# Preparing the first y and gate tiles within the scan stage, and holding a quarter of a long convolution's taps back behind the first attention heads, in a two-block kernel

## The chip, the cores and the metric

The kernel runs on one core of a Trainium2 chip. The metric is device time in microseconds for one execution; the figure given for a kernel is the median of several. Besides the timed runs there is one profiled execution, with a time of its own, from which all rows below are read. Engines: PE is TensorE's matrix products, PEld its weight loads, DVE is VectorE, ACT is ScalarE, POOL is GpSimd, SP is SyncE, which here issues all transfers.

## What is computed

A sequence of 512 tokens with 1024 features passes through two blocks. The first has an RWKV-7 mixer and a short-convolution mixer, the second a branch with a 31-tap causal depthwise convolution beside stick-breaking attention, then a feed-forward part. What the change touches is this:

```python
# first block, RWKV-7 mixer, after the scan over chunks and the group norm
y = (y + bonus.reshape(bsz, t, D_INNER)) * jax.nn.silu(g.astype(f32))
out = y.astype(h.dtype) @ w_out                    # 512x2048 @ 2048x1024
...
# second block
u = jax.nn.glu(conv_in, axis=-1)
u = causal_depthwise_conv(u, conv_dw_w, conv_dw_b) # 31 taps, 512 channels
u = jax.nn.silu(layernorm(u, conv_ln_g, conv_ln_b))
conv_out = jnp.einsum('bsc,cd->bsd', u, w_conv_branch) + b_conv_branch
att = stick_breaking_attention(q, k, v)            # 8 heads of 64, 128-row query blocks
att_out = jnp.einsum('bsc,cd->bsd', att, w_att_branch)
merged = jax.nn.sigmoid(g_conv) * conv_out + jax.nn.sigmoid(g_att) * att_out
```

## The kernel before

Every dense product is done with both operands split into a high and a low part (`split`, L175 to L178: ScalarE casts the high part at L176, VectorE subtracts it at L177), and three matmuls per pair of tiles: high by high, high by low, low by high. A weight chunk of 128 x 1024 numbers is fetched by SyncE (`Products.fetch`, L60), cast by ScalarE (L65), and its low part made by POOL in two halves (L73). TensorE's three matmuls are L85 to L87 in `dense_feat` and L119 to L121 in `dense_tok`.

The program has stages one after the other. `scan_phase` runs the chunked scan over 8 pairs of head tiles (q = 0 to 7); it lists operations with a cost, a due time and dependencies, and `list_schedule` orders them over the engines. Pair q stores two tiles of y, 128 x 512 each, to `yD` (L1408). In between, 16 gate tiles are computed (L1466 to L1473) and stored to `sgD` (L1476). The gate products read `xg`, which fills the shared slots 2 and 3 until the last of them; the slots 0 and 1 hold the scan's `g` by turns.

`post_phase` begins with the output projection. `prep(c)` (L1793) loads two of the sixteen tiles of y and of the gate (`yl`, `gl`, L1796, three buffers each), multiplies them on VectorE (L1797) and splits the product into `y2`: the first eight tiles lie in slots 2 and 3, the others in `yb`. `out_proj` calls it before each weight chunk, runs a first pass of 16 row tiles (12 matmuls each) over half of the output columns, and a second pass over the other half. At c = 2 prep also issues the loads of the norm's gain and of x (L1659, L1802).

Later `post_phase` does the long convolution (L1877 to L1889): for each of four channel tiles the GLU product goes to `up`, one instruction starts `conv` with tap 0 (L1884), and thirty more add a tap each on VectorE (L1887). `attention` (L2021) takes eight heads. `scores(hd)` makes z = k q^T (L2035), then on ScalarE Abs, Exp and Ln (L2042 to L2044), on VectorE ez (L2046), on POOL the mask (L2047), and the split into `sp` (L2049, L2050). `weights(hd)` adds the running sums of sp to z (L2064), then VectorE takes a minimum (L2067), ScalarE exponentiates (L2068, L2070), VectorE masks (L2071), and `pat` collects the values (L2072). The buffer of ez is doubled, so the third and fourth blocks of a head wait for the first two.

Between these steps stand fillers, other work for TensorE: g is a gate product (24 matmuls), b a convolution branch (12), n the convolution's layer norm, a its activation. A string for each head says what comes ahead of the next head's scores, ahead of the weights, and behind them. The engines' queues are in order; the framework's own scheduler merges the calls into one order for each engine.

Of the kernel before, what the change touches and what calls it, by code (L numbers as in the profile page):

```python
# [17 lines left out]
P = 128  # L18
T = 512
NT = T // P  # L20
D = 1024
KD = D // P
DI = 2048
KI = DI // P

C = 64
NC = T // C
# [4 lines left out]
CW2 = 31  # L32
# [120 lines left out]
def two_block_kernel(ctx, tc, A, out):  # L153
    nc = tc.nc
# [104 lines left out]
    with ExitStack() as rk_ctx:  # L259
# [28 lines left out]
        shared = dict(xg=[], VU=[])  # L288
# [303 lines left out]
def emit_ops(nc, tc, ops, bufs):  # L592
    ET = mybir.EngineType
    order = list_schedule(ops, bufs)
    with tc.manual_schedule(engines={ET.PE, ET.DVE, ET.Activation, ET.Pool, ET.SP}):
        for o in order:
            o["fn"]()
# [486 lines left out]
def scan_phase(nc, tc, A, E):  # L1084
# [5 lines left out]
    op = L.op  # L1090
    Q = KI // 2
    with ExitStack() as s:
# [402 lines left out]

        for q in range(Q):
            build(q)
        gate()
        emit_ops(nc, tc, L, dict(KB=2, ZR=4, V=1, VU=4, m=3, G=4, KBT=4, wy=1, UU=2, **INVERSE,
# [136 lines left out]
def post_phase(ctx, tc, A, out, E):  # L1636
# [147 lines left out]
    with ExitStack() as s:  # L1784
        gp = s.enter_context(tc.tile_pool(name="gp", bufs=1))
        ep = s.enter_context(tc.tile_pool(name="ep", bufs=1))
        gain = gain_tile(ep, "b_norm", load=False)
        ya = (slot(2), slot(3))
        yb = tuple(gp.tile([P, KD, T], F32R, tag=f"yb{i}", name=f"yb{i}") for i in range(2))
        y2 = tuple(rows(a) + rows(b) for a, b in zip(ya, yb))  # L1790

        def prep(c):
            for i in (2 * c, 2 * c + 1):  # L1793
                y, g = (ep.tile([P, T], F32, tag=n, name=n, bufs=3) for n in ("yl", "gl"))
                for t, src in ((y, yD), (g, sgD)):
# [60 lines left out]
    with ExitStack() as s:  # L1856
# [8 lines left out]
        with tc.tile_pool(name="mq", bufs=1) as mq:  # L1865
# [12 lines left out]
            vt = mq.tile([P, NT, T], F32, tag="vt", name="vt")  # L1878
            for i in range(4):
# [6 lines left out]
                for tap in range(1, CW2):  # L1886
                    nc.vector.scalar_tensor_tensor(out=conv[:, i, :], in0=up[:, i, tap:tap + T],  # L1887
                                                   scalar=col("conv_dw_w_2", tap * 4 + i), in1=conv[:, i, :],
                                                   op0=ALU.mult, op1=ALU.add)  # L1889
# [48 lines left out]
            def conv_branch(i):  # L1938
# [6 lines left out]
            todo = dict(g=gates, b=branches, n=iter([conv_norm]), a=iter([conv_act]))  # L1945
            filler = [[[next(todo[q]) for q in part] for part in head.split(",")] for head in
                      ("ggg,g,", ",ng,", "a,g,g", ",g,bb", ",g,b", ",g,ggbb", ",g,gb", ",g,gbb")]
# [72 lines left out]
def attention(nc, tc, E):  # L2020
    qT, kT, vt, at, mq, bank, filler = (E[k] for k in ("qT", "kT", "vt", "at", "mq", "bank", "filler"))  # L2021
# [4 lines left out]
    def scores(hd):  # L2026
# [4 lines left out]
        for i in (0, 1, 3, 2):  # L2031
# [18 lines left out]
            nc.vector.tensor_tensor(out=lo, in0=sp, in1=hi.bitcast(F32), op=ALU.subtract)  # L2050
        heads[hd] = zs, sps

    def weights(hd):
# [6 lines left out]
        for i in range(NT):  # L2060
# [10 lines left out]
            nc.vector.tensor_tensor(out=a[:, 0:P], in0=a[:, 0:P], in1=cmask, op=ALU.mult)  # L2071
# [41 lines left out]
```

## Time and profile before

| | us |
|---|---|
| timed runs, median (lowest to highest of 3) | 2073.43 (2072.57 to 2083.99) |
| profiled execution, its own time | 2071.24 |
| its span, first to last instruction | 2069.5 |
| busy: PE / DVE / ACT / POOL | 1967.4 / 1046.2 / 838.8 / 760.7 |
| mean granted TensorE clock | 0.980 |

The span lies inside the execution's own time, 1.7 us shorter. Times of rows count from the span's start. A clock of 1.00 in a row is TensorE's higher level, 2.4 GHz, and 0.50 the lower, 1.2 GHz; values between are stretches with both. A matmul's row shows its length with pipelining, so one that follows another starts earlier than the other's end. The chain of work that ended last is 77% PE and 13% DVE, the convolution's taps alone 6%.

### The profile page before, as it was taken

Reading aid. Unit: us, or ns where it says so; the run is one execution under the profiler, and the core shown is the slowest. Engines: PE = TensorE matmul, PEld = TensorE weight load, DVE = VectorE, ACT = ScalarE, POOL = GpSimd, SP = SyncE. Lnnn points to the kernel's source line nnn. Section 1 sums busy time; section 2 is a strip of 40 time slices with the busy share of each in tenths; the row PEclk is TensorE's granted clock in tenths of the full one; section 3 lists DMA queues with packets and bytes.
Section 4 is the critical chain, followed back from the end, with each engine's and each line's share of the span. In section 5 each row is a group of like instructions: output and inputs, shape, how many; then the busy total and the mean of one; then the engine's idle time right before and its main releaser. Section 6 shows DMA issues by size and latency. Waiting matters only on the chain.

```text
span 2069.5 us, 37138 instructions
## 1 busy us (share of the span) xinstructions
PE 1967.4 (95%) x15076; PEld 1579.5 (76%) x15076; DVE 1046.2 (51%) x2007; ACT 838.8 (41%) x1637; POOL 760.7 (37%) x660
## 2 busy tenths in 40 slices
PE   6989999799999979999999999996999999999998
PEld 5768888587778758888888887884667778888886
DVE  7958987688785342432332313797552442111101
ACT  5444554376655632322222223323765343223221
POOL 4220000001001135555555556753233565544442
PEclk9999999899999989999999999998999999999999
DMA  4445555634443383333333333331111523333321
GB/s 150 121 167 184 190 191 174 184 115 147 142 131 105 107 285 113 89 96 93 98 95 93 100 114 102 112 93 45 33 50 51 167 73 102 92 94 100 102 93 70
DMA packets 285763, 241.14 MB, mean 117 GB/s; under 512 B 14520, under 2 KB 236056, under 8 KB 285592
## 3 DMA queue, kind: packets, MB, share of 16 engines
q1 hardware_dynamic: 285592, 238.77, 37.2%
q8 instruction: 118, 1.93, 0.4%
q14 instruction: 53, 0.43, 0.1%
HBM read 198.89 MB, written 39.85 MB: 115 GB/s over the span
## 4 chain that ended last, share of the span: by engine, by line
PE 77%; DVE 13%; DMA 3%; issue 3%; ACT 2%; POOL 2%; SPq 0%; DVEq 0%; POOLq 0%; ACTq 0%
PE b L86 11%; PE b L85 11%; PE b L87 11%; PE b L120 6%; PE b L121 6%; DVE conv L1887 6%; PE b L119 5%; PE ps_d L940 3%; PE ps_d L941 3%; PE ps_d L942 3%; PE wy L1206 2%; PE us L1206 2%; PE ps_g L1466 1%; DVE X L662 1%; DVE xtmp L654 1%
## 5 line engine op out<-in xcount | busy, mean ns | idle before, releaser
L73 POOL TENSOR_TENSOR wl<-wr,wh 128x512 fp32r<-128x512 f32 (+1 forms) x463 | 641.4, 1408 | 615.1 <-ACT wh L65 613.8
L65 ACT CAST wh<-wr 128x1024 fp32r<-128x1024 f32 (+1 forms) x241 | 245.5, 1020 | 706.7 <-PE b L86 475.2
L87 PE MATMUL b<-s,wl 128*128 128x512 f32 x1024 | 404.1, 395 | 0.0
L86 PE MATMUL b<-s,wh 128*128 128x512 f32 x1024 | 404.0, 395 | 0.0
L85 PE MATMUL b<-s,wh 128*128 128x512 f32 x1024 | 403.1, 394 | 0.0
L85 PEld LDWEIGHTS b<-s,wh 128*128 128x128 f32 x1024 | 192.6, 188 | 47.0 <-issue 1.5
L86 PEld LDWEIGHTS b<-s,wh 128*128 128x128 f32 x1024 | 192.7, 188 | 45.7 <-issue 1.4
L87 PEld LDWEIGHTS b<-s,wl 128*128 128x128 f32 x1024 | 192.9, 188 | 43.6 <-issue 0.8
L119 PE MATMUL b<-wh,s 128*128 128x512 f32 x288 | 115.1, 400 | 13.9 <-ACT s L176 13.9
L1887 DVE SCALAR_TENSOR_TENSOR conv<-up,pkC,conv 128x512 f32<-128x512 f32 x120 | 117.1, 1042 | 0.4
L1359 POOL TENSOR_SCALAR var<-var 128x8 f32<-128x8 f32 x16 | 4.7, 293 | 305.9 <-ACT scr L1352 305.9
L120 PE MATMUL b<-wl,s 128*128 128x512 f32 x288 | 114.7, 398 | 0.0
L121 PE MATMUL b<-wh,s 128*128 128x512 f32 x288 | 111.1, 397 | 0.0
L2006 DVE TENSOR_TENSOR a<-sg,b 128x512 f32<-128x512 f32 x22 | 15.1, 688 | 172.5 <-PE b L87 164.3
L119 PEld LDWEIGHTS b<-wh,s 128*128 128x128 f32 x288 | 54.8, 190 | 27.8 <-ACT s L176 15.0
L1827 DVE TENSOR_TENSOR cu<-b,us 128x512 f32<-128x512 f32 x16 | 11.1, 692 | 124.3 <-PE b L87 119.0
L869 POOL MEMSET sg<- 128x8 f32 x16 | 1.7, 112 | 180.8 <-ACT pcl L893 162.7
L662 DVE TENSOR_TENSOR X<-X,xtmp 128x120 f32<-128x120 f32 (+24 forms) x248 | 65.0, 262 | 6.0
L654 DVE TENSOR_TENSOR xtmp<-dn,X 128x120 f32<-128x120 f32 (+24 forms) x248 | 64.8, 261 | 5.9
L121 PEld LDWEIGHTS b<-wh,s 128*128 128x128 f32 x288 | 54.8, 190 | 13.1
L120 PEld LDWEIGHTS b<-wl,s 128*128 128x128 f32 x288 | 54.8, 190 | 12.9
L1466 PE MATMUL ps_g<-xg_hi,wh 128*128 128x512 f32 x128 | 58.7, 459 | 2.0 <-ACT sgt L1473 2.0
(346 smaller groups left out, 4132.5 us busy)
## 6 DMA issues: line engine op xcount, KB each, us to landing
wr<-in_a_w_in SPq DMA_DIRECT2D x64, 512.0 KB, 4.6
wr<-in_b_w_in SPq DMA_DIRECT2D x64, 512.0 KB, 4.1
wr<-in_w_ffn_up SPq DMA_DIRECT2D x44, 512.0 KB, 3.9
wr<-in_w_in SPq DMA_DIRECT2D x36, 512.0 KB, 3.7
wr<-in_w_ffn_down SPq DMA_DIRECT2D x22, 512.0 KB, 3.5
kbD<-KB SPq DMA_DIRECT2D x16, 512.0 KB, 2.8
zrD<-ZR SPq DMA_DIRECT2D x16, 512.0 KB, 3.4
KB<-kbD SPq DMA_DIRECT2D x16, 512.0 KB, 4.5
```

What stands on the lines that cost most here:

```text
L65: copy = self.nc.scalar.copy(out=hi[:, :n], in_=raw[:, :n])
L73: eng.tensor_tensor(out=lo[:, sl], in0=raw[:, sl], in1=hi[:, sl].bitcast(F32), op=ALU.subtract)
L85: nc.tensor.matmul(ps, wh[:, k, :], xh[k], start=k == 0, stop=False)
L86: nc.tensor.matmul(ps, wh[:, k, :], xl[k], start=False, stop=False)
L87: nc.tensor.matmul(ps, wl[:, k, :], xh[k], start=False, stop=k == nk - 1)
L119: nc.tensor.matmul(pss[t], th, wh[:, k, :], start=s, stop=False)
L120: nc.tensor.matmul(pss[t], th, wl[:, k, :], start=False, stop=False)
L121: nc.tensor.matmul(pss[t], tl, wh[:, k, :], start=False, stop=e)
L654: nc.vector.tensor_tensor(out=tmp(i), in0=S["dn"][:, :, i:i + 1, 0:i].to_broadcast([P, 2, w, i]), in1=S["X32"][:, :, c:, i:i + 1].to_broad ...
L662: nc.vector.tensor_tensor(out=X, in0=X, in1=tmp(i), op=ALU.subtract)
L1206: nc.tensor.matmul(out, lhs, rhs, start=start, stop=True, skip_group_check=True)
L1887: nc.vector.scalar_tensor_tensor(out=conv[:, i, :], in0=up[:, i, tap:tap + T], scalar=col("conv_dw_w_2", tap * 4 + i), in1=conv[:, i, :], ...
```

## The change

There are two parts. In the scan stage a new `first_rows` loads the first four tiles of y and gate into slot 0, after the last use of that slot by pair 6, multiplies them on VectorE, and, after the last gate product has read slots 2 and 3, splits them into these slots. `prep` then does only tiles 4 to 15. In the second block the thirty taps of the fourth channel tile no longer follow its tap 0; six fillers c of five taps each are called in heads 0 to 2, and a tap may stand on VectorE only behind the last `sp` or mask operation that was called before it (`mark`). The layer norm n moves from head 1 to head 3, the activation a from head 2 to head 4, and gates and branches are dealt anew.

```diff
+        def first_rows():
...
+                    for b, src in enumerate((yD, sgD)):
+                        nc.sync.dma_start(out=S["in"][:, 2 * i + b, :], in_=src[i * P:(i + 1) * P, :])
...
+                    nc.vector.tensor_tensor(out=y, in0=y, in1=S["in"][:, 2 * i + 1, :], op=ALU.mult)
...
+                    nc.scalar.copy(out=made[0][:, i, :], in_=S["in"][:, 2 * i, :])
...
+                    nc.vector.tensor_tensor(out=made[1][:, i, :], in0=S["in"][:, 2 * i, :],
+                                            in1=made[0][:, i, :].bitcast(F32), op=ALU.subtract)
...
+            for i in range(4):
+                op("SP", 0.4, ld(i), 40 + i, ("y", "ld", i), [(Q - 2, "y_add", NC - 1)] + ([("y", "ld", 0)] if i else []),
+                   dma=2.0)
+                op("DVE", 0.69, gated(i), 40 + i, ("y", "gated", i), [("y", "ld", i)])
+                op("ACT", 0.6, high(i), 40 + i, ("y", "high", i),
+                   [("y", "gated", i), (100 + KI - 1, "dense", 7)] + ([("y", "high", 0)] if i else []))
+                op("DVE", 0.69, low(i), 40 + i, ("y", "low", i), [("y", "high", i)])
...
-        ya = (slot(2), slot(3))
+        ya = E["shared"]["y2"]
...
-            for i in (2 * c, 2 * c + 1):
+            for i in (2 * c, 2 * c + 1) if c > 1 else ():
...
+            def taps(i, which):
+                for tap in which:
+                    y = nc.vector.scalar_tensor_tensor(out=conv[:, i, :], in0=up[:, i, tap:tap + T],
...
+                    if mark:
+                        after(y, mark[-1])
...
-                for tap in range(1, CW2):
-                    nc.vector.scalar_tensor_tensor(out=conv[:, i, :], in0=up[:, i, tap:tap + T],
-                                                   scalar=col("conv_dw_w_2", tap * 4 + i), in1=conv[:, i, :],
-                                                   op0=ALU.mult, op1=ALU.add)
+                if i < 3:
+                    taps(i, range(1, CW2))
...
+            rest = iter([partial(taps, 3, range(t, t + 5)) for t in range(1, CW2, 5)])
...
-                      ("ggg,g,", ",ng,", "a,g,g", ",g,bb", ",g,b", ",g,ggbb", ",g,gb", ",g,gbb")]
+("ggg,cg,c", "c,cg,g", "c,cg,g", ",ng,g", "a,g,g", ",g,bbg", ",g,bbb", ",g,bbb")]
...
-            nc.vector.tensor_tensor(out=lo, in0=sp, in1=hi.bitcast(F32), op=ALU.subtract)
+            mark.append(nc.vector.tensor_tensor(out=lo, in0=sp, in1=hi.bitcast(F32), op=ALU.subtract))
...
-            nc.vector.tensor_tensor(out=a[:, 0:P], in0=a[:, 0:P], in1=cmask, op=ALU.mult)
+            mark.append(nc.vector.tensor_tensor(out=a[:, 0:P], in0=a[:, 0:P], in1=cmask, op=ALU.mult))
```

How the order moves, at three places. SyncE in the last pair of the scan, as a piece of the difference (L1505 are the new loads, L1476 a gate store, L1445 the last gate tile's weights, L743 V, L1408 the y store of pair 6):

```order
-L1476 DMA sgD<-sgt 128x512
-L1445 DMA wr<-in_a_w_in 128x8x128
-L743 DMA V<-vD 64x4x128 x4
+L1505 DMA y_in<-yD 128x512
+L1505 DMA y_in<-sgD 128x512
+L1476 DMA sgD<-sgt 128x512
+L1505 DMA y_in<-yD 128x512
+L1505 DMA y_in<-sgD 128x512
+L1445 DMA wr<-in_a_w_in 128x8x128
+L1505 DMA y_in<-yD 128x512
+L1505 DMA y_in<-sgD 128x512
+L743 DMA V<-vD 64x4x128 x4
```

Three of the four pairs of loads stand ahead of the V loads; the fourth follows them, and the y stores of pairs 6 and 7 come later still.

ScalarE at the end of the scan (L1473 evicts the last gate tile, L1397 scales the last rows of y, L1519 is the new cast of the high part, L176 the cast in `prep`):

```order
 L65 CAST wh<-wr 128x1024 x2
 L1473 ACTIVATE sgt<-ps_g 128x512
-L1397 ACTIVATE yo<-tY,pkB 128x256 x2
-L176 CAST s_9868<-yl 128x512 x3
```

That is the order before: no cast of a y tile ahead of the last rows of y, and `prep` begins with tile 0. The same place in the change:

```order
+L1519 CAST y_hl_9843<-y_in 128x512
+L1397 ACTIVATE yo<-tY,pkB 128x256 x2
+L1519 CAST y_hl_9843<-y_in 128x512 x3
+L176 CAST y_hl_9843<-yl 128x512
+L65 CAST wh<-wr 128x1024
```

One new cast goes ahead of the last rows of y, three behind them, and the first cast in `prep` is now that of tile 4.

VectorE at the first attention head, before (L1887 taps, L2046 ez, L2050 the low part of sp):

```order
1474 L1884 TENSOR_SCALAR conv<-up,pkC,pkB 128x512
1475 L1887 SCALAR_TENSOR_TENSOR conv<-up,pkC,conv 128x512 x82
1476 L2046 SCALAR_TENSOR_TENSOR ez<-z,ez 128x512
1477 L2046 SCALAR_TENSOR_TENSOR ez<-z_14578,ez 128x384
1478 L2050 TENSOR_TENSOR sp_14588<-ez,sp_14587 128x512
```

All taps of the block stand ahead of the first ez. In the change, at the same place (L1925 taps, L2097 ez, L2101 the low part, L2118 the minimum, L2122 the mask):

```order
1479 L1936 TENSOR_SCALAR conv<-up,pkC,pkB 128x512
1480 L1925 SCALAR_TENSOR_TENSOR conv<-up,pkC,conv 128x512 x52
1481 L2097 SCALAR_TENSOR_TENSOR ez<-z,ez 128x512
1482 L2097 SCALAR_TENSOR_TENSOR ez<-z_14541,ez 128x384
1483 L2101 TENSOR_TENSOR sp_14551<-ez,sp_14550 128x512
```

The block ahead of the first ez is 30 taps shorter. Where the 30 stand now, a piece from heads 1 and 2:

```order
1502 L2101 TENSOR_TENSOR sp_14737<-ez,sp_14736 128x256
1503 L1925 SCALAR_TENSOR_TENSOR conv<-up,pkC,conv 128x512
1504 L2122 TENSOR_TENSOR ea<-ea,cmask 128x128
1505 L1925 SCALAR_TENSOR_TENSOR conv<-up,pkC,conv 128x512 x2
1506 L2097 SCALAR_TENSOR_TENSOR ez<-z,ez 128x512
1507 L1925 SCALAR_TENSOR_TENSOR conv<-up,pkC,conv 128x512
1508 L2097 SCALAR_TENSOR_TENSOR ez<-z_14834,ez 128x384
1509 L1925 SCALAR_TENSOR_TENSOR conv<-up,pkC,conv 128x512
1510 L2101 TENSOR_TENSOR sp_14844<-ez,sp_14843 128x512
```

They stand one to three at a time behind the last low part of head 1's scores (row 1502), the last of them behind the weights of head 2.

## Rows read from the trace of the kernel before

**Rows 1.** List of waits of the whole execution: waiting engine and line, total us, times, longest.

```profile
PE z L2035 <- DVE ez L2046: 21.6, 2, 20.6
PE b L119 <- ACT s L176: 13.9, 3, 11.3
```

**Rows 2.** Timeline of TensorE, 727 to 789: start us, us, instruction, idle before and its releaser.

```profile
727.29 0.33 PE L1383 MATMUL tY<-ident,Y 128*128 128x128 f32 x1 [0.33 <-ACT Y L1367]
738.89 0.79 PE L119 MATMUL b<-wh,s 128*128 128x512 f32 x1 [11.27 <-ACT s L176]
744.07 0.39 PE L119 MATMUL b<-wh,s 128*128 128x512 f32 x1
755.52 0.51 PE L119 MATMUL b<-wh,s 128*128 128x512 f32 x1 [1.70 <-ACT s L176]
788.92 0.39 PE L119 MATMUL b<-wh,s 128*128 128x512 f32 x1
```

**Rows 3.** Timeline of ScalarE, VectorE and SyncE, 729 to 738, same columns.

```profile
729.51 1.00 ACT L1397 ACTIVATE yo<-tY,pkB 128x256 f32<-128x256 f32 x2
730.10 0.88 DVE L1403 TENSOR_TENSOR yo<-tV,yo 128x256 f32<-128x256 f32 x2 [9.51 <-ACT yo L1397]
737.45 0.69 DVE L1797 TENSOR_TENSOR yl<-yl,gl 128x512 f32<-128x512 f32 x1 [6.48 <-DMA gl<-sgD]
733.65 0.32 SPq L1796 DMA_DIRECT2D yl<-yD  x1
```

**Rows 4.** Table by stage: stretch, length, busy by engine, granted clock, DMA share, GB/s.

```profile
730.00:745.00 15.00, 6.11 (x17) 4.84 (x18) 4.85 (x8) 2.37 (x5) 3.17 (x3) 0.54 0.94 319
745.00:755.00 10.00, 7.86 (x33) 5.75 (x31) 2.83 (x4) 2.77 (x4) 2.96 (x2) 1.00 1.01 380
```

**Rows 5.** Timeline of VectorE in the last pair's scan, one step of eight.

```profile
692.75 0.29 DVE L1263 TENSOR_TENSOR UU<-us,sums 128x128 f32<-128x128 f32 x1 [1.97 <-PE us L1206]
```

**Rows 6.** VectorE's taps: chain, timeline, and table by stage (PE, PEld, DVE, ACT, POOL).

```profile
1312.58 1.69 DVE conv L1887
...
1358.14 45.30 DVE L1887 SCALAR_TENSOR_TENSOR conv<-up,pkC,conv 128x512 f32<-128x512 f32 x43
...
1410.08 21.90 DVE L1887 SCALAR_TENSOR_TENSOR conv<-up,pkC,conv 128x512 f32<-128x512 f32 x32
...
1358.10:1403.40 45.30, 45.30 (x194) 36.14 (x193) 45.30 (x45) 13.30 (x18) 25.64 (x16) 1.00 0.33 100
```

**Rows 7.** TensorE at the first attention head: timeline, and table by stage.

```profile
1433.10 0.79 PE L2035 MATMUL z<-qT,kT 64*128 64x128 f32 x2 [20.64 <-DVE ez L2046]
...
1436.00:1438.00 2.00, 2.00 (x8) 1.58 (x8) 0.00 (x0) 1.97 (x8) 1.78 (x2) 0.79 0.00 0
```

**Rows 8.** The attention stage: table by stage, and groups of instructions over 1420 to 1660.

```profile
1450.00:1475.00 25.00, 24.62 (x116) 16.70 (x116) 16.84 (x47) 16.53 (x45) 8.13 (x14) 1.00 0.08 22
...
L2050 DVE TENSOR_TENSOR sp<-ez,sp 128x512 fp32r<-128x512 f32 (+3 forms) x32 | 20.2, 645 | 8.1 <-ACT sp L2049 7.9
L2046 DVE SCALAR_TENSOR_TENSOR ez<-z,ez 128x512 f32<-128x512 f32 (+3 forms) x32 | 15.1, 485 | 26.9 <-ACT ez L2044 26.8
L2071 DVE TENSOR_TENSOR ea<-ea,cmask 128x128 f32<-128x128 f32 x32 | 15.1, 476 | 8.0 <-ACT ea L2068 7.8
L2067 DVE TENSOR_SCALAR ea<-z 128x128 f32<-128x128 f32 x32 | 9.3, 290 | 37.0 <-PE z L2064 23.1 <-PE pat L2072 13.9
L2072 PE MATMUL pat<-ea,vt 128*64 128x512 f32 (+3 forms) x64 | 25.0, 481 | 0.2 <-DVE ea L2071 0.2
L2035 PE MATMUL z<-qT,kT 64*128 64x128 f32 (+3 forms) x58 | 21.7, 485 | 22.1 <-DVE ez L2046 21.6 <-DVE ea L2067 0.5
L2064 PE MATMUL z<-sp,tri_neg 128*128 128x512 f32 (+3 forms) x64 | 19.2, 363 | 0.0
L2064 PE MATMUL z<-sp,ones_neg 128*128 128x128 f32 (+2 forms) x96 | 17.5, 284 | 0.0
```

**Rows 9.** Table by stage in the fourth head.

```profile
1516.00:1518.00 2.00, 2.00 (x3) 0.44 (x3) 2.00 (x2) 0.59 (x3) 2.00 (x3) 0.50 0.00 0
```

More of the change, by code (lines that the diff above doesn't have):

```diff
@@ L287, in two_block_kernel @@
         iv = rk_ctx.enter_context(tc.tile_pool(name="iv", bufs=1))
-        shared = dict(xg=[], VU=[])
+        shared = dict(xg=[], VU=[], y2=[])
         chunk_phase(nc, tc, A, locals())
@@ L1494, in gate, with ld, go, gated @@
                 tile_ops(i)
+        def first_rows():
+            S, made = {}, E["shared"]["y2"]
+            def ld(i):
+                def go():
+                    if i == 0:
+                        S["in"] = rc.tile([P, KD, T], F32, tag="s0", name="y_in")
+                    for b, src in enumerate((yD, sgD)):
+                        nc.sync.dma_start(out=S["in"][:, 2 * i + b, :], in_=src[i * P:(i + 1) * P, :])
+                return go
+            def gated(i):
+                def go():
+                    y = S["in"][:, 2 * i, :]
+                    nc.vector.tensor_tensor(out=y, in0=y, in1=S["in"][:, 2 * i + 1, :], op=ALU.mult)
+                return go
+            def high(i):
+                def go():
+                    if i == 0:
+                        for b in range(2):
+                            made.append(rc.tile([P, KD, T], F32R, tag=f"s{2 + b}", name=f"y_hl{b}"))
+                    nc.scalar.copy(out=made[0][:, i, :], in_=S["in"][:, 2 * i, :])
+                return go
+            def low(i):
+                def go():
+                    nc.vector.tensor_tensor(out=made[1][:, i, :], in0=S["in"][:, 2 * i, :],
+                                            in1=made[0][:, i, :].bitcast(F32), op=ALU.subtract)
+                return go
+            for i in range(4):
[5 more added lines that the diff above has]
+                op("DVE", 0.69, low(i), 40 + i, ("y", "low", i), [("y", "high", i)])
         for q in range(Q):
@@ L1498, in scan_phase @@
         gate()
+        first_rows()
         emit_ops(nc, tc, L, dict(KB=2, ZR=4, V=1, VU=4, m=3, G=4, KBT=4, wy=1, UU=2, **INVERSE,
@@ L1878, in post_phase @@
             vt = mq.tile([P, NT, T], F32, tag="vt", name="vt")
+            mark = []
+            def taps(i, which):
+                for tap in which:
+                    y = nc.vector.scalar_tensor_tensor(out=conv[:, i, :], in0=up[:, i, tap:tap + T],
+                                                       scalar=col("conv_dw_w_2", tap * 4 + i), in1=conv[:, i, :],
+                                                       op0=ALU.mult, op1=ALU.add)
+                    if mark:
+                        after(y, mark[-1])
             for i in range(4):
@@ L1944, in post_phase @@
             branches = iter([partial(conv_branch, i) for i in range(KD)])
-            todo = dict(g=gates, b=branches, n=iter([conv_norm]), a=iter([conv_act]))
+            rest = iter([partial(taps, 3, range(t, t + 5)) for t in range(1, CW2, 5)])
+            todo = dict(g=gates, b=branches, c=rest, n=iter([conv_norm]), a=iter([conv_act]))
             filler = [[[next(todo[q]) for q in part] for part in head.split(",")] for head in
-                      ("ggg,g,", ",ng,", "a,g,g", ",g,bb", ",g,b", ",g,ggbb", ",g,gb", ",g,gbb")]
+("ggg,cg,c", "c,cg,g", "c,cg,g", ",ng,g", "a,g,g", ",g,bbg", ",g,bbb", ",g,bbb")]
             attention(nc, tc, locals() | E)
@@ L2020, in attention @@
 def attention(nc, tc, E):
-    qT, kT, vt, at, mq, bank, filler = (E[k] for k in ("qT", "kT", "vt", "at", "mq", "bank", "filler"))
+    qT, kT, vt, at, mq, bank, filler, mark = (E[k] for k in ("qT", "kT", "vt", "at", "mq", "bank", "filler", "mark"))
     tri_neg, ones_neg, cmask, split, table, after = (E[k] for k in ("tri_neg", "ones_neg", "cmask", "split", "table",
```

## Prediction

> **What bounds the kernel now.** I read the list of waits first, because TensorE is busy nearly all the time and only its few long waits can be won. Two single waits stand out [rows 1]: one of 20.6 us for VectorE at the first attention head (z of L2035, behind ez of L2046), and one of 11.3 us for ScalarE at the head of the first output projection (L119, behind the cast of L176). The timelines around the two places then say what ended each wait, and the table by stage says what the clock did.
>
> The first place [rows 2]: the scan's last transposes end at 727.62, and the projection starts at 738.89. Between them ScalarE and VectorE finish the last rows of y, y is stored, the loads of y and gate go out behind that store at 733.65, their gating starts at 737.45, and only the cast after it lets TensorE go [rows 3]. The granted clock is then 0.54 over 730 to 745 [rows 4], the lower level, 1.2 GHz, for over half of that stretch. Two smaller waits for the same loads follow. From 755.52 to 788.92 the pass is unbroken: 12 of its 16 row tiles in 33.40 us, 2.78 us a tile [rows 2]. The transfers bind in the middle: 319 GB/s over 730 to 745 and 380 over the ten us behind, with the queues busy 0.94 and 1.01 of the time [rows 4].
>
> The second place: VectorE runs the 120 taps of the long convolution in one block that ends at 1431.98 [rows 6], and the first head's ez, in program order behind them, is what z waits for until 1433.10 [rows 7]. TensorE has nothing else it may do, since its queue is in order.
>
> **The change, part one: four y tiles in the scan.** Eight loads move out of the projection's head into the last pair of the scan. They are past the point where they could wait for the last y store, since SyncE's order has them ahead of it. SyncE's issues are 0.32 to 0.43 us each (the row of 733.65 is one), about 3 us for eight; behind them on SyncE stand a gate store, the last gate weights and the V loads, so these may go out some 3 us later in sum, spread over three places. VectorE gets four products of 0.69 us in the scan's steps. It sits idle 1.97 us in front of a scan product there [rows 5], so each fits; if a load were late, the scan step behind it would wait as long. I take nought, between a loss of 3 us (four products all in the way) and a gain of 1 us (VectorE's order now has one scan step ahead of a product that waits for V).
>
> At the end, four casts of 0.62 us and four low parts of 0.69 us (those of the rows behind 737.45) wait for the last gate matmul, whose input lies in the slots that they write. One cast stands ahead of the last two ScalarE operations on y, so these move from 729.51 to 730.1, and VectorE's additions from 730.10 to 730.7, ending at 731.6 with their 0.88 us [rows 3]. TensorE's first product waits for VectorE and starts at about 731.8, not 738.89; it needs only tile 0, and the three other tiles, 0.62 us of ScalarE each, stay ahead of its 2.78 us a tile. Its wait is still some 4 us, so I let the clock drop as it did before: 12 products then took from 738.89 to 744.07, 5.2 us in place of 2.8, a loss of 2.4. I keep that loss whole (bounds 0 and 2.4).
>
> Tiles 0 to 3 last until 731.8 + 4 x 2.78 + 2.4 = 745.3, tiles 4 and 5 until 750.9. Their loads start where those of tiles 0 and 1 did, half a us later, and were through in 4 us then. Tile 6 comes behind one weight chunk, four loads of y and gate, the gain, four loads of x and its own two: 4.5 MB from about 733.5, at 319 GB/s over 14 us, so by 748, gated and cast by 750. It is about in time; I take 0.7 us of waiting, between 0 and 5 (the far bound is a rate of some 230 GB/s, under both stretches of [rows 4]). From there a tile with its half chunk of weights is 0.75 MB per 2.78 us, 270 GB/s, below what the queues moved. The pass ends at 731.8 + 16 x 2.78 + 2.4 + 0.7 = 779.4 in place of 788.92: **9.5 us** less, bounds 4 and 12.5.
>
> **Part two: thirty taps behind the first heads.** With POOL idle the last 32 taps take 21.90 us, 0.684 each. So the last 30 start at 1431.98 - 30 x 0.684 = 1411.4 [rows 6]; that is when VectorE now comes to the head's ez. The two ez that TensorE waits for take to 1412.6, and z goes at 1412.8 in place of 1433.10. ScalarE and POOL sat idle behind the same wait, and their next casts and low parts start as much earlier. That is **20.3 us**. Behind the old wait the clock was still at the lower level until about 1436.8 (0.79 over 1436 to 1438 [rows 7]), half of 3.7 us: **1.9 us** more, since the new wait is under half a us.
>
> What comes back: 30 taps among the operations of heads 1 to 3, between the last scores of head 1 and the last weights of head 2. VectorE's own work there is two heads. The four lines of a head (L2050, L2046, L2071, L2067) sum to 59.7 us for eight heads, 7.5 us a head [rows 8]. A tap beside POOL is dearer: 43 taps took 45.30 us where POOL was busy 25.64 of 45.30 us, 1.05 each against 0.684 [rows 6]. Linear in POOL's share, 0.33 in the heads [rows 8], a tap is 0.684 + 0.37 x 0.33/0.57 = 0.90 us. Sum for VectorE: 27 + 15 = 42 us. TensorE in that stretch has four gate products of 24 matmuls at 0.232 us (2.78 over the 12 of a tile), 22.3, and two heads at (25.0 + 21.7 + 19.2 + 17.5)/8 = 10.4 us, 43 in all [rows 8]. So the two engines are level, and the cover is thin. VectorE enters with a lead, because a gate of 5.6 us stands on TensorE ahead of what reads head 1's last scores. I take 1.5 us of new waits, between 0 and 23 (below).
>
> The gates and branches are also dealt anew: a head has at least two of the 5.6 us gates as cover, where head 1 had one gate and head 4 one and a half. Around 1516 the before ran at a clock of 0.50 [rows 9] after waits of under 1 us; such a loss is some 4 to 5 us. It may go, stay or come elsewhere, since branches move late: I take 1.5 us gained, between a gain of 5 and a loss of 3.
>
> A rule speaks against this part. The rows say 1.05 us beside a POOL busy 0.57 of the time [rows 6], which is 0.62 of POOL's time added to VectorE's. The Trainium skill (SBUF — State Buffer, section Who interferes with whom) says that a VectorE instruction with two SBUF inputs and a GpSimd instruction that reads SBUF exclude each other: whichever starts first holds the port for its whole length. By that rule all of POOL's time would be added, a tap would be 0.684/0.67 = 1.02 us, VectorE's sum 45.6 and the total some 2 to 3 us later; the trace agrees in kind and not in full.
>
> **Sum.** 9.5 + 20.3 + 1.9 - 1.5 + 1.5 = 31.7 us. Against the profiled execution's 2071.24 us that is 2039.5; against the median of the runs shown, 2073.43, which is 2.2 above it, 2041.7. I forecast **2041** for a median.
>
> **The rivals.**
> 1. VectorE becomes the bound in heads 1 to 3. For it: 42 against 43 us, and the first taps of the block, beside an always busy POOL, took 1.69 us (one of four alike stands in [rows 6]). At that price it is 50.7 + 15 = 65.7 us, 22.7 over TensorE's 43; at 1.05 it is 3.6 over. Against it: POOL's share there is 0.33. Middle: 12 us back, 2053. Chance 0.16.
> 2. The transfers keep the gain of part one. For it: the queues were full from 730 to 755 [rows 4], and x and the gain still stand ahead of tile 6. With tile 6 some 5 us late part one is 4: 2047. Against it: 2 MB less in that stretch. Chance 0.13.
> 3. The wait at the first head is only passed on: its chain (three ScalarE passes, ez, mask, cast, low part, twice for want of buffers) becomes the wait once VectorE is free. Half of the 20.3 us comes back: about 2052 to 2055. Against it: after 1433.10 TensorE ran on without a wait over the same chain. Chance 0.03.
> 4. Slower: taps in front of each head's operations make TensorE stop for under 1 us again and again, as around 1516, and the clock stays at 1.2 GHz through all of that stretch. Its 43 us of work then cost 86: 2041 + 43 = 2084. It decides once the lower level holds for over 32 us of work. Against it: the old gaps there lasted one head. Chance 0.02.
> That the change does not act is excluded by the order: loads and taps stand where the diff says.
>
> **How the numbers follow.** Forecast 0.66, with an own range of 2033 to 2050; rivals 0.16, 0.13, 0.03 and 0.02. The range of 2030 to 2058 takes in the gains' far bounds below (12.5, and 5 more in the late heads) and most of rival 1 above. One per cent, 20.7 us, is about what a measurement of this kernel can tell from no change: under 2052.7 lie nearly all of the forecast and of rival 2 and half of rival 1, 0.85; within one per cent 0.13; slower 0.02.
>
> **What would show it.** Right: a first projection matmul near 732, second pass at about 779; no wait over 2 us for ez at the first head, taps ending near 1402 (1411.4 less 9.5), and TensorE near full over the next three heads. Wrong: a long wait of L119 for y tiles 6 or 7; VectorE at 0.95 or more with TensorE waiting for sp or ea through heads 1 to 3; a clock of 0.50 in windows there; a scan that ends later than 727.6.

## The result and the profile after

The changed kernel took 2043.86 us (median of 4 runs, 2039.32 to 2045.16), the kernel before 2074.09 in the runs beside it (2072.57 to 2083.99): a ratio of 0.9838, 95% interval 0.9820 to 0.9856, some 30 us or 1.6% less. Forecast were 2041 and a range of 2030 to 2058. The profiled execution has a span of 2041.8 us and took 2043.54.

From the list of waits of the changed kernel over the whole execution, the rows of the projection and of the attention; columns as in [rows 1]:

```profile
PE b L119 <- DVE yo L1403: 4.5, 1, 4.5
...
PE b L119 <- ACT y_hl L176: 2.0, 1, 2.0
...
PE pat L2123 <- DVE ea L2122: 0.9, 1, 0.9
PE z L2086 <- DVE ez L2097: 0.8, 1, 0.8
```

Both long waits of [rows 1] are gone. At the head of the first projection TensorE waits 4.5 us where it waited 11.3, and no longer for a y tile but for its own PSUM bank, which VectorE's last addition of y frees. At the first attention head it waits 0.8 us for ez where it waited 20.6.

The timeline of TensorE around the projection, against [rows 2]:

```profile
729.01 0.33 PE L1383 MATMUL tY<-ident,Y 128*128 128x128 f32 x1 [0.34 <-ACT Y L1367]
733.83 0.77 PE L119 MATMUL b<-wh,y_hl 128*128 128x512 f32 x1 [4.49 <-DVE yo L1403]
755.58 0.50 PE L119 MATMUL b<-wh,y_hl 128*128 128x512 f32 x1 [1.98 <-ACT y_hl L176]
824.72 1.03 PE L1724 MATMUL tp<-ident,xg 128*128 128x128 f32 x8
```

The last row is the first transpose behind the whole projection, the same point in both programs. In the kernel before it is this one:

```profile
828.64 0.60 PE L1683 MATMUL tp<-ident,xg 128*128 128x128 f32 x4
```

So the profile has only 3.9 us gained at the end of the projection. But the scan ended at 729.34 here and at 727.62 before. From the end of the scan to that transpose it is 95.38 us against 101.02: part one gained 5.6 us in this pair of profiles, and 1.7 us of it are covered by a scan that was longer in this execution. Ten profiles of kernels with the early y tiles (this one and nine of those below) have the scan's end between 724.54 and 735.07, mean 729.4; the two without have it at 727.62 and 730.39. The early loads and products do not cause the delay. At the same transposes, about when the first early load goes out (675.67 in the kernel before, 678.01 here), the changed kernel was already 2.3 us late. From there to the scan's end it took 51.3 us, the kernel before 52.0; in the other kernels with early tiles that stretch is 50.0 to 51.5 us, in part two alone 52.4. From here on the places are measured each from its own start.

Why it is 5.6 and not more shows in the other engines' timelines (ScalarE, VectorE, SyncE) of the changed kernel over the same stretch:

```profile
728.87 1.97 ACT L65 CAST wh<-wr 128x1024 fp32r<-128x1024 f32 x2
730.75 0.58 ACT L1473 ACTIVATE sgt<-ps_g 128x512 f32<-128x512 f32 x1
731.74 1.01 ACT L1397 ACTIVATE yo<-tY,pkB 128x256 f32<-128x256 f32 x2
...
731.87 1.14 DVE L1524 TENSOR_TENSOR y_hl<-y_in,y_hl 128x512 fp32r<-128x512 f32 x1 [9.27 <-ACT y_hl L1519]
732.94 0.74 DVE L1403 TENSOR_TENSOR yo<-tV,yo 128x256 f32<-128x256 f32 x2
754.18 0.69 DVE L1838 TENSOR_TENSOR yl<-yl,gl 128x512 f32<-128x512 f32 x1 [6.09 <-DMA gl<-sgD]
...
738.75 0.32 SPq L1837 DMA_DIRECT2D yl<-yD  x1
741.01 3.08 SPq L1843 DMA_DIRECT2D x_sb<-in_x  x4
745.03 0.67 SPq L1837 DMA_DIRECT2D gl<-sgD  x1
```

And the chain of waits there, start and length of each piece:

```profile
733.81 4.80 DMA yD<-yo
738.75 4.09 DMA yl<-yD
...
745.03 9.12 DMA gl<-sgD
```

In the kernel before, the first of these pieces reads:

```profile
731.00 2.51 DMA yD<-yo
```

One of the new low parts (731.87) stands ahead of VectorE's last additions of y, so the store behind these is issued later. It lands 4.80 us after its issue and not 2.51, and the load of tile 4 is released by that landing, at 738.75, 9.4 us behind the scan's end; in the kernel before, the first load of y went out 6.0 us behind it [rows 2, 3]. Then come the gain and the four loads of x, and only then tile 6, whose gate needs 9.12 us to land. TensorE has done tiles 0 to 5 by then and waits 1.98 us. The table by stage, columns as in [rows 4], shows what both waits cost beyond themselves:

```profile
733.80:740.30 6.50, 6.47 (x16) 5.12 (x17) 3.19 (x3) 0.50 (x1) 2.04 (x2) 0.53 0.81 260
740.30:747.30 7.00, 7.00 (x32) 5.68 (x31) 2.22 (x4) 2.19 (x3) 1.17 (x1) 1.00 0.83 280
757.00:760.50 3.50, 3.50 (x11) 2.68 (x10) 3.50 (x3) 1.12 (x2) 2.68 (x2) 0.52 0.97 341
```

The granted clock is 0.53 behind the first wait and 0.52 again behind the second, the lower level, 1.2 GHz. I add up, in steps of 1 us, the length times one minus the clock: 3.0 us lost behind the first wait and 1.7 behind the second. Waits and lost clock taken away, the projection is 84.2 us long here, 84.6 in the kernel before, and between 83.6 and 85.2 in all kernels below: waits and clock make up all but 0.4 us of the difference between the two.

The first attention head, from the timelines of VectorE and TensorE:

```profile
1384.86 23.35 DVE L1925 SCALAR_TENSOR_TENSOR conv<-up,pkC,conv 128x512 f32<-128x512 f32 x23
1408.13 1.15 DVE L2097 SCALAR_TENSOR_TENSOR ez<-z,ez 128x512 f32<-128x512 f32 x2
...
1409.34 0.49 PE L2086 MATMUL z<-qT,kT 64*128 64x128 f32 x2 [0.81 <-DVE ez L2097]
```

The block of taps ends at 1408.1 in place of 1431.98. Where the 30 held taps stand, the group of taps reads (count, busy us, mean ns of one, idle before):

```profile
L1925 DVE SCALAR_TENSOR_TENSOR conv<-up,pkC,conv 128x512 f32<-128x512 f32 x30 | 26.3, 875 | 0.3
```

And the table by stage over that stretch:

```profile
1434.90:1476.50 41.60, 41.60 (x172) 27.30 (x172) 37.49 (x65) 26.76 (x65) 16.33 (x16) 1.00 0.11 33
```

TensorE is busy for all of the 41.60 us and VectorE for 37.49 of them.

The mean of 875 ns hides two kinds of tap. From the list of the tile conv (count, then shortest, median and longest in ns), the 30 held taps, and the last 32 of the block in the kernel before, beside which POOL stood idle:

```profile
L1925 DVE SCALAR_TENSOR_TENSOR conv<-up,pkC,conv x30: 737/746/1795, 1435.0 to 1474.8; 128x512 f32<-128x512 f32 x30
L1887 DVE SCALAR_TENSOR_TENSOR conv<-up,pkC,conv x32: 737/738/752, 1410.1 to 1431.2; 128x512 f32<-128x512 f32 x32
```

And two pairs of rows from the timelines of VectorE and POOL in the changed kernel:

```profile
1443.71 0.74 DVE L1925 SCALAR_TENSOR_TENSOR conv<-up,pkC,conv 128x512 f32<-128x512 f32 x1
1443.77 1.84 POOL L73 TENSOR_TENSOR wl<-wr,wh 128x512 fp32r<-128x512 f32 x1 [3.70 <-ACT wh L65]
...
1445.58 1.34 POOL L73 TENSOR_TENSOR wl<-wr,wh 128x512 fp32r<-128x512 f32 x1
1445.68 1.78 DVE L1925 SCALAR_TENSOR_TENSOR conv<-up,pkC,conv 128x512 f32<-128x512 f32 x1
```

Of the 30 held taps 25 took 0.74 to 0.75 us, as with POOL idle. The other five took 0.90 to 1.80; each began while a POOL instruction was running and ended 0.55 us behind that one's end. So it is with all 42 long taps among this kernel's 120 and all 37 among those of the kernel before; the rest took 0.73 to 0.75 us. A tap that began first, as at 1443.71, lost nothing, and POOL's instruction beside it took 1.84 us, the next one 1.34.

From the head's first z to the first transpose of the normalisation behind the attention's output projection the changed kernel takes 257.48 us, the kernel before 281.01: part two gained 23.5 us. The stretch between the two places (573.48 us against 573.49) and the one behind, to the end of the last matmul (379.29 against 379.50), are equal within 0.3 us. So -1.7 + 5.6 + 23.5 + 0.2 = 27.6 of the 27.7 us between the two spans.

### The profile page after: what moved, and what is told of

It reads as the page before. It is cut to its first block, busy times and chain, and to the rows that moved or that the text cites. A ratio compares the mean times of both kernels' runs of the same rounds, so it can differ in the third digit from the quotient of the medians.

```text
span 2041.8 us, 37143 instructions
## 1 busy us (share of the span) xinstructions
PE 1965.1 (96%) x15076; PEld 1578.2 (77%) x15076; DVE 1047.2 (51%) x2007; ACT 837.1 (41%) x1637; POOL 764.0 (37%) x660
## 4 chain that ended last, share of the span: by engine, by line
PE 82%; DVE 9%; DMA 3%; issue 2%; ACT 2%; POOL 2%; SPq 1%; DVEq 0%; POOLq 0%; ACTq 0%
PE b L87 12%; PE b L85 12%; PE b L86 12%; PE b L120 6%; PE b L121 6%; PE b L119 5%; PE ps_d L940 3%; PE ps_d L941 3%; PE ps_d L942 3%; DVE conv L1925 3%; PE wy L1206 2%; PE us L1206 2%; PE ps_g L1466 1%; PE z L2115 1%; PE ps_g L1162 1%
## 5 line engine op out<-in xcount | busy, mean ns | idle before, releaser
L1925 DVE SCALAR_TENSOR_TENSOR conv<-up,pkC,conv 128x512 f32<-128x512 f32 x120 | 123.4, 1074 | 0.7
L119 PE MATMUL b<-wh,s 128*128 128x512 f32 x224 | 88.6, 396 | 0.0
L120 PE MATMUL b<-wl,s 128*128 128x512 f32 x224 | 88.5, 395 | 0.0
L121 PE MATMUL b<-wh,s 128*128 128x512 f32 x224 | 88.5, 395 | 0.0
L1812 DVE TENSOR_TENSOR gm<-b,norm_ffn_post 128x512 f32<-128x512 f32 x8 | 5.5, 692 | 108.3 <-ACT scr L1714 108.3
L1876 DVE TENSOR_TENSOR cv<-cv,b 128x512 f32<-128x512 f32 x16 | 11.0, 688 | 94.4 <-PE b L87 94.3
L101 PE MATMUL b<-s,wh 128*128 128x256 f32 x192 | 55.1, 290 | 4.4 <-DVE s L1728 4.4
```

The lines of the kernel that those rows point to most:

```text
L119: nc.tensor.matmul(pss[t], th, wh[:, k, :], start=s, stop=False)
L120: nc.tensor.matmul(pss[t], th, wl[:, k, :], start=False, stop=False)
L121: nc.tensor.matmul(pss[t], tl, wh[:, k, :], start=False, stop=e)
L1925: y = nc.vector.scalar_tensor_tensor(out=conv[:, i, :], in0=up[:, i, tap:tap + T], scalar=col("conv_dw_w_2", tap * 4 + i), in1=conv[:, i, ...
```

## The experiments

The theory after the result: the two parts are independent; part one is cut short by tile 6 and the clock, part two is what was forecast. One table for all; "head" is TensorE's wait ahead of the first product, "later" its waits in the rest of the projection, "A" the time from the scan's end to the transposes behind the projection, "B" from the first z to the transposes behind the attention's output projection, all in us of the profiled execution; the time is the median of the runs. The times come from four sets of runs: the kernel before took 2074.09 us beside the change, 2075.33 beside the next four, 2077.53 beside the four behind those, and 2074.55 beside the last two.

| kernel | head | later | A | B | time |
|---|---|---|---|---|---|
| before | 11.27 | 2.66 | 101.02 | 281.01 | 2074.09 |
| the change | 4.49 | 1.98 | 95.38 | 257.48 | 2043.86 |
| part one alone | 4.56 | 2.90 | 93.50 | 280.67 | 2070.61 |
| part two alone | 11.03 | 3.87 | 102.60 | 257.54 | 2052.40 |
| x behind the tiles | 4.48 | 1.02 | 92.87 | 257.47 | 2044.81 |
| chunks behind the tiles | 4.48 | 1.88 | 94.42 | 257.48 | 2043.35 |
| held taps left out | 4.48 | 1.74 | 93.36 | 256.99 | 2042.90 |
| 45 taps held | 4.48 | 3.20 | 94.11 | 262.67 | 2048.28 |
| heads with one gate | 4.48 | 3.13 | 96.64 | 266.38 | 2055.68 |
| new dealing alone | 4.48 | 3.14 | 96.46 | 278.27 | 2067.07 |
| the change again | 4.48 | 3.01 | 95.40 | 257.52 | 2045.61 |
| x and casts late | 2.00 | 0 | 86.30 | 257.45 | 2037.07 |

**The parts apart.** Part one alone (the taps and the old dealing put back) and part two alone (no early tiles):

```diff
-                if i < 3:
-                    taps(i, range(1, CW2))
+                taps(i, range(1, CW2))
...
-        first_rows()
```

> Part one alone: four y tiles in the scan, all 120 taps in the block and the gates and branches dealt as before. Theory (the y tiles gain 3.9 us because the tiles behind them come late, and the two parts are independent): 2070 us, some 4 under before, first output projection over 3.9 us earlier than in before, the 20.6 us wait at the first head there again. Rival (the small gain came from something that the taps' part does to the first projection): 2064 to 2065, the 9.5 us of the prediction.

Measured: 2070.61 us, ratio 0.9970 (0.9953 to 0.9987), beside 2075.33 for the kernel before. The wait of 20.5 us at the first head is there again. But its first projection was over 10.6 us earlier than in the kernel before, as its scan ended 3.1 us earlier; A is 7.5 us shorter. So the 3.9 us in that expectation were a wrong reading of one pair of profiles.

> Part two alone: 30 taps held back and the new dealing of gates and branches, no y tiles in the scan. Theory: 27.4 - 3.9 = 23.5 us under before, 2050 us, with 19.9 us of it at the first head. Rival (part two gains by the earlier start that part one gives): over 2053.

Measured: 2052.40 us, ratio 0.9883 (0.9856 to 0.9910), 22.9 us less; B is 257.54, within 0.06 of the change. The second part does not need the first. In the medians part one is worth 4.7 us by itself and 7.3 beside part two (30.2 less 22.9).

**What makes tile 6 late.** In the first of these the gain and x go behind tiles 7 to 15, in the second weight chunks 4 to 6 go behind tile 5:

```diff
-            if c == 2:
-                load_gain(gain, "b_norm")
-                for t in range(NT):
-                    nc.sync.dma_start(out=x_sb[:, t, :], in_=x_v[:, t, :])
+            if c == 3:
+                after(load_gain(gain, "b_norm"), last)
+            if c > 3:
+                after(nc.sync.dma_start(out=x_sb[:, c - 4, :], in_=x_v[:, c - 4, :]), last)
```

> The change, with the loads of the gain and of x (2.5 MB) taken from behind tile 5 and put one at a time behind tiles 7, 9, 11, 13 and 15. Theory A (x ahead of tile 6 on SyncE's queue makes tile 6 late): the wait of 1.98 us for tile 6 goes and the stretch at the lower clock behind it too (about 1.6 us): first projection 3.6 us shorter, 2040. Theory B (the late landing of the last y store starts every later load late, x matters little): the wait stays above 1 us. Theory C (the transfers as a whole bind): the wait only moves to a later tile, no gain.

The waits inside the projection of this kernel, from the list of waits over that stretch:

```profile
PE b L119 <- ACT yb L176: 0.8, 2, 0.6
PE b L121 <- DVE yb L177: 0.2, 1, 0.2
```

The wait for tile 6 is gone (the first later one is 0.57 us, 42 us into the projection), the lower clock behind it too, and A is 2.5 us shorter than in the change, though the load of tile 4 went out later still, 10.6 us behind the scan's end. Theory A holds, with 2.5 us in place of the 3.6 expected. The median, 2044.81, doesn't show it: what is gained is less than what executions differ by (the scan of this profile alone ended 4.5 us later than that of the change).

> The change, with the weight chunks 4, 5 and 6 of the first projection (0.5 MB each), which SyncE issues ahead of and around the last y store, put behind the loads of tiles 4 and 5; x stays where it is. Theory B (the chunks' packets hold up the y store, which took 4.8 us from its issue to the first dependent load, against some 2.3 us in before): the load of tile 4 goes 2 to 2.5 us earlier (738.75 to about 736.5), tile 6 as much earlier, its wait of 1.98 us is gone or under 0.3: 2040 to 2042. Theory A (x decides): the wait stays above 1.5 us and the time is that of the change, 2044.

The timeline of SyncE in this kernel:

```profile
735.04 0.81 SPq L1411 DMA_DIRECT2D yD<-yo  x2
740.07 0.32 SPq L1841 DMA_DIRECT2D yl<-yD  x1
```

And the table by stage between the two rows:

```profile
737.00:739.00 2.00, 2.00 (x6) 1.56 (x5) 1.65 (x2) 0.00 (x0) 0.50 (x1) 0.50 0.14 48
739.00:741.00 2.00, 2.00 (x8) 1.60 (x7) 0.00 (x0) 0.00 (x0) 0.00 (x0) 0.80 0.01 4
```

No chunk stands around the store now and the DMA engines are nearly idle (0.14 and 0.01), yet the load still goes out 5.0 us after the store's first issue, and the wait stays at 1.88 us. The gain that theory B promised does not come. But the trace doesn't clear the chunks; it shows a second cause behind them. From the list of transfers of this kernel, over 735 to 740 and then over 738.3 to 740:

```profile
q8 instruction: 1, 0.02, 2.2%
...
DMA packets 9, 0.02 MB, mean 10 GB/s; under 512 B 1, under 2 KB 1, under 8 KB 9
```

The trace records the landing of the store's second half in 16 parts. In the kernel before and in part two alone all of them land 2.3 to 2.5 us after its issue. Here 15 land 2.1 to 2.3 us after it, by 737.73, and the last at 739.86. The first row is one packet of 16 KB of the kind "instruction", from 736.63 to 738.37. The nine of the second row follow its end one by one until 739.39 and are all that still moves, so the store's last part seems to have stood behind that packet. Each of the ten kernels with early tiles has one such packet between the store's issue and its landing, and a last part that lands 0.4 to 2.1 us behind the other 15; the two kernels without have no such packet there, their next one of that size begins some 17 us behind the scan's end. In the change, where the chunks do stand around the store, the first 15 parts land 3.1 to 4.4 us after the issue and the last 4.8. So by the records the chunks hold up most of the store and the instruction packet the last of it, and taking the chunks away alone gains next to nothing. No run moved the packet, so this second cause is read from the traces and not tested.

**What the held taps cost.**

```diff
-            rest = iter([partial(taps, 3, range(t, t + 5)) for t in range(1, CW2, 5)])
+            rest = iter([partial(taps, 3, ()) for t in range(1, CW2, 5)])
```

> The change without the 30 held taps: the fourth quarter of the long convolution keeps its first tap only, the other 30 are not computed; all else as in the change. Theory (TensorE is the bound in heads 1 to 3 and VectorE only level with it): from the first head's z to the first transposes behind the output projection of attention 257.5 - 1 us, since the one wait of 0.95 us for the mask goes; time within 2 us of the change, 2042 to 2044. Rival (VectorE decides in heads 1 to 3, waits that show as slower TensorE and not as idle): 252 us or less there, under 2039.

Measured: B 256.99, 0.5 us less, and a median of 2042.90. The 26.3 us of held taps cost half a us: TensorE covers them.

In the next, fifteen more taps are held:

```diff
-                if i < 3:
-                    taps(i, range(1, CW2))
+                if i < 3:
+                    taps(i, range(1, CW2 if i < 2 else 16))
...
-("ggg,cg,c", "c,cg,g", "c,cg,g", ",ng,g", ...
+("ggg,ccg,c", "cc,cg,g", "cc,cg,g", ",ng,g", ...
```

> The change with 45 taps held back instead of 30: the last 15 of the third quarter are dealt between heads 0 and 2 too, the block is 75 taps. Theory (a held tap costs VectorE 0.9 us beside its other work, and VectorE had 8.6 us idle of 50 in heads 1 to 3): 15 taps more are 13.4 us, 5 over what is idle; nothing is won at the first head, whose wait was 0.8 us. Waits of 4 to 8 us in sum in heads 1 to 3 and some 2 to 5 us at the lower clock: 2050 to 2057. Rival (VectorE still hidden, since later heads give it time): within 2 us of the change. Rival at the price of 1.69 us a tap: 25 us more of VectorE, 2060 or more.

The waits of the first heads in its list:

```profile
PE z L2116 <- ACT ea L2122: 2.1, 1, 2.1
PE b L85 <- DVE yn L1971: 1.5, 1, 1.5
PE lnp L1963 <- ACT ea L2122: 0.5, 1, 0.5
```

And the table by stage around the end of the longest:

```profile
1464.90:1467.10 2.20, 0.10 (x2) 0.04 (x1) 2.20 (x3) 2.20 (x9) 1.95 (x2) 1.00 0.00 0
1467.00:1472.00 5.00, 4.78 (x12) 3.10 (x13) 5.00 (x14) 2.41 (x9) 1.87 (x2) 0.66 0.19 56
```

B is 5.2 us longer and the time 2048.28, just under the expected 2050 to 2057. VectorE is busy for all of the 2.20 us in which TensorE waits and for all of the 5.00 us behind, in which TensorE runs at 0.66. So the cover ends between 30 and 45 taps. The 45 held taps took 0.87 us each in the mean, near the 0.9 of the theory and far from 1.69.

**What the new dealing is worth.** Once with one gate in heads 1 and 3, once with the taps back in the block:

```diff
-("ggg,cg,c", "c,cg,g", "c,cg,g", ",ng,g", "a,g,g", ",g,bbg", ",g,bbb", ",g,bbb")]
+("ggg,cg,c", "c,cg,", "c,cg,g", ",ng,", "a,g,g", ",g,bb", ",g,ggbbb", ",gg,bbb")]
```

> The change with the gates and branches dealt so that heads 1 and 3 have one gate of 5.6 us and not two (two gates go to head 5 and one each stands elsewhere: ggg,cg,c / c,cg, / c,cg,g / ,ng, / a,g,g / ,g,bb / ,g,ggbbb / ,gg,bbb). Theory (the second gate is the cover of a head): waits of 1 to 4 us in head 1 or 3, and a stretch at the lower clock behind them, 4 to 8 us more from the first head's z to the transposes behind the attention's output projection: 261 to 266 in place of 257.5. Rival (the dealing makes no odds as long as the taps are held): 257 to 259.

Its longest waits in the attention, from the list of waits:

```profile
PE z L2086 <- DVE ez L2097: 2.0, 3, 1.0
PE z L2115 <- DVE sp L2101: 1.9, 1, 1.9
```

And the table by stage around two of them:

```profile
1468.00:1474.00 6.00, 5.30 (x15) 3.44 (x16) 5.83 (x15) 3.31 (x12) 1.35 (x2) 0.72 0.15 44
1537.00:1549.00 12.00, 11.01 (x22) 5.40 (x23) 5.47 (x16) 7.21 (x21) 3.34 (x6) 0.57 0.15 44
```

B is 8.9 us longer, 266.38, a little over the 4 to 8 expected: waits of 1.9 us early and 1.0 us later on, and a clock of 0.57 over the 12 us around the second, where the kernel before had its own such stretch [rows 9].

> The change with all 120 taps back in the block ahead of the first head, but the new dealing of gates and branches kept. Theory (of the 23.5 us of part two 19.8 are the wait, some 1.5 the clock behind that wait, and some 2.2 the small waits and the stretch at the lower clock in the fourth head, which the new dealing removes): from the first head's z 281.0 - 2.2 = 279 us, 2064 to 2066 in all. Rival (the new dealing does nothing by itself): 281. Rival (the held taps themselves cost TensorE some us): 277 or less.

Measured: B 278.27, 2.7 us under that of the kernel before where 2.2 were expected, with the wait of 20.52 us in place and no stretch at the lower clock in the later heads; 2067.07 us in all. The new dealing by itself is worth 2.7 us, the held taps 20.8.

**A version that beats both.** The change again beside a kernel with x behind the tiles and with two of ScalarE's casts moved:

```diff
+        M.hold = lambda copy: after(copy, E["shared"]["high"]) if M.count in (13, 14) else None
         ws = out_proj(A["a_w_out"][0], y2, KI, *residual_norm(ep, gain, hl1, late), z_srcs(0), prep=prep)
+        M.hold = None
```

E["shared"]["high"] is the last of the four new casts, and 13 and 14 number weight chunks 1 and 2.

> The change once more, beside the next kernel on the same chip: 2044 us; from the end of the scan to the first transpose behind the first projection 93.5 to 95.4 us, as its own profile and that of part one alone had it.

> The change with two edits: the gain and x behind tiles 7 to 15, as in the run before of that kind, and ScalarE's casts of weight chunks 1 and 2 (1.97 us, ahead of the last gate tile and the last rows of y) put behind the four new casts of y. Theory: the casts stood in the chain to TensorE's first product (gate tile, y rows, bank free), so the wait at the projection's head falls from 4.48 to some 2.5 us; tile 6 does not wait; with the lower clock for some 2 us behind the first wait that is 90 to 91 us from the end of the scan to the first transpose behind the projection, 4 under the change: 2039 to 2041. Rival (the casts are needed as early as they stood: TensorE waits for chunk 1 or 2): a wait of over 1 us at tile 2 or 4 and no gain over the x edit alone, 92.9.

The change again took 2045.61 us with an A of 95.40; the version took 2037.07, ratio to the kernel before 0.9823 (0.9808 to 0.9838). Its timelines of ScalarE and TensorE:

```profile
724.29 0.57 ACT L1473 ACTIVATE sgt<-ps_g 128x512 f32<-128x512 f32 x1
727.73 2.95 ACT L65 CAST wh<-wr 128x1024 fp32r<-128x1024 f32 x3
...
726.91 0.47 PE L119 MATMUL b<-wh,y_hl 128*128 128x512 f32 x1 [2.00 <-DVE yo L1403]
```

And its table by stage from the scan's end on:

```profile
724.90:740.00 15.10, 13.10 (x57) 10.65 (x57) 7.61 (x12) 7.97 (x13) 8.01 (x6) 1.00 0.69 228
740.00:760.00 20.00, 20.00 (x87) 16.07 (x86) 10.98 (x12) 7.93 (x10) 15.38 (x10) 1.00 1.04 387
```

The gate tile's eviction now follows the scan's last rows directly, the bank comes free 2.0 us after the last transpose, and behind this wait the clock stays at 1.00, which I had not counted on: A is 86.30 in place of 95.40, 9.1 us less (2.5 of waiting at the head, 3.0 for tile 6, the rest the clock). The transfers run at 387 GB/s there and TensorE doesn't wait for them.

## Why the prediction was right, and where not

**The time was right, and part two with it, step by step.** VectorE was to come to the head's ez at 1411.4, less what the stages ahead give. They gave 3.9 us in this profile, so 1407.5; measured 1408.1. The wait of 20.64 us fell to 0.81, 19.8 us against 20.3 forecast. Behind it the granted clock is 1.00, as said. The block's price of 0.684 a tap held for those that left, since they had run with POOL idle [rows 6].

**The price of the held taps came out near, but not by the forecast's mechanism.** It was forecast at 0.90 us for a POOL share of 0.33; the mean was 0.875 at a share of 0.39 (16.33 of 41.60 us). The two are not of one kind: the 0.684 and 1.05 behind the forecast are steps from tap to tap, 0.875 is the mean length of one, which is 0.74 with POOL idle. POOL added 0.13 us a tap, some 4 us in all, where the forecast had 0.22, 6.5 in all. Nor was it in proportion to POOL's share: five taps paid it, those that began while POOL was running, and 25 paid nothing. That the mean came so near is in part luck. The rule of the Trainium skill (SBUF — State Buffer, section Who interferes with whom) is that a VectorE instruction with two SBUF inputs and a GpSimd instruction that reads SBUF exclude each other. The rows of the taps bear it out instruction by instruction, so "in kind and not in full" was a wrong reading: what fails is to add all of POOL's time, which by the same estimate would be 0.684/(1 - 0.39) = 1.12 us a tap here, since POOL waits too when the tap began first (1443.77).

The 1.5 us of waits that I took for the held taps were half a us (the run without them), and the 42 us of VectorE against 43 of TensorE came out at 37.5 busy of 41.6. Rival 1 did not happen, and the run with 45 taps shows how near it was: at 15 taps more VectorE decides.

**The new dealing was forecast at 1.5 us and measured 2.7,** from the cause that was named: a head with one gate pays with a wait and the lower clock (8.9 us in the run that took the gates away).

**Part one was mis-sized: 9.5 us forecast, 5.6 measured** in the profile (A of the seven kernels with the same code there is 93.4 to 96.6, mean 95.0; of the two without early tiles 101.0 and 102.6). It is rival 2's mechanism with under rival 2's loss. The steps, as the prediction put them:
- TensorE's first product "starts at about 731.8", 4.1 us behind the scan's end: 4.49. Right, but for 0.4: VectorE takes the first of the four low parts (731.87) ahead of the additions, and the prediction had none there.
- "I keep that loss whole" (2.4 at the lower clock): 3.0 in this profile, 1.6 to 2.7 in the others.
- "Their loads start where those of tiles 0 and 1 did, half a us later": this step failed. They started 3.4 us later (9.4 against 6.0), because the store that they wait for was issued 1.1 us later and took 4.80 us, not 2.51. The prediction let the store land as it had before; the traces show the chunks around it and one instruction packet in its way.
- Tile 6: "It is about in time; I take 0.7 us of waiting, between 0 and 5": 1.98 in this profile, 1.7 to 3.2 in the others. It follows from the step above and from x: with x and the gain out of the way it is gone, though the load of tile 4 went out later still.
- The lower clock behind that second wait, 1.7 us, had no term at all.

0.4 + 0.6 + 1.3 + 1.7 is 4.0, the missing 3.9 us but for rounding. Over all such profiles part one gained somewhat more: the means of A are 95.0 and 101.8, a gain of 6.8; the medians gave 4.7 and 7.3. Forecast for both parts were 31.7 us; the medians have 30.2, the two profiles 27.7. Part two came out 1.3 us above its 22.2 and part one 3.9 below its 9.5, so in part the total is near because two errors went opposite ways.

My list of what would prove the prediction wrong had "a scan that ends later than 727.6" and "a long wait of L119 for y tiles 6 or 7". The first was no test, since the scan's end differs by 10.5 us between executions; the second came true at 2 us.

## What to carry to other kernels

A block of work that only has to be done some time later should not stand in an engine's queue ahead of what TensorE waits for next: deal it out behind stretches where TensorE has work of its own, and find the point where the cover ends by adding half as much again. When the first loads of a stage are moved ahead, the next ones inherit their place: ask what they wait for (here the landing of a store) and take bulk that nobody needs yet, such as x here, out from between. Where an instruction's mean price depends on what another engine does, look at its shortest, median and longest before a formula is laid through the mean. A gain of a few us is read place by place from the trace, from each place's own start, since another stage may vary by more than that from execution to execution.

## What was not expected of the hardware

- The scan ended between 724.54 and 735.07 us after the start in twelve profiles, with the same code up to its last pair. Aligned instruction by instruction, the two extremes (part one alone and the heads with one gate) are within 1.2 us of each other until 495 us, drift 8.8 us apart between there and 616 in steps of at most 1.7 us, and keep that distance to within 0.8 us until the end.
- The length of a wait alone doesn't decide whether the clock falls. Behind waits for tile 6 of 1.88, 1.98, 3.01 and 3.13 us it fell to 0.50, for 3.5 to 7 us; behind others of 1.74, 2.90 and 3.20 us, and behind 2.00 us at the head of the last version, it stayed at 1.00. The wait of 2.90 us is in part one alone, at 750.38, and the table by stage has for the stretch behind it:

```profile
750.40:756.00 5.60, 5.60 (x24) 4.42 (x25) 5.24 (x6) 2.13 (x3) 3.14 (x2) 1.00 1.00 356
```

- The store of the last y rows, 0.5 MB in two parts, let the loads behind it go 3.1 us after its first issue in the kernel before and in part two alone, and 4.6 to 6.6 us after it in the kernels with early tiles. With the DMA engines otherwise idle, the last of the 16 parts of its second half, behind one packet of 16 KB of the kind "instruction", landed 1.7 and 2.1 us after the other 15 (the last version, and the chunks behind the tiles).
- POOL does not slow a tap on VectorE little by little. A tap that begins with POOL free took 0.73 to 0.75 us; one that takes longer began while a POOL instruction was running and ended 0.55 us behind that one's end (37 taps of 120 in the kernel before, 42 in the change).
